# Plain fp32 products of the attentions held for a companion, and a charge for each change of product kind in the build's estimate

## The chip, the cores and the metric

The kernel runs on one core of one Trainium2 chip. The metric is device time in microseconds (us), and lower is better. In the text TensorE (PE) makes the matrix products, with its weight loads listed apart (PEld); VectorE is DVE, ScalarE is ACT, GpSimd is POOL, and SP is the engine whose queue starts most of the DMA transfers.

## The reference

One step of a one-layer decoder, on a prompt of 512 tokens and on 8 samples of 4 new tokens each, with the same weights. All data are fp32. Cut to what matters here:

```
z = rmsnorm(x) @ w_in                       # 2048 -> 7712 columns: q, k, v, gates
# group A, 8 heads, 2 shared k/v heads: native sparse attention
kc, vc = compress(rows of k, v)             # one row for each 32 tokens
o_A = g0*softmax(q kc) vc + g1*softmax(q k_selected) v_selected + g2*softmax(q k_window) v_window
# group B, 8 heads: forgetting attention
s[t, u] = q[t].k[u]/sqrt(128) + D[t] - D[u],  D = cumsum(log sigmoid(...))
o_B = softmax(s) v
y = rmsnorm(x + concat(o_A*silu(z_A), o_B*silu(z_B)) @ w_out)
```

The prompt attends to itself. A sample attends also to 1024 past tokens, which lie in pages of 128 rows in a shared cache and are found by a page table. The projected k and v, the logs of the forgetting gates and the new windows are outputs too.

## The kernel before

**The products.** The kernel has two kinds of matrix product. The projections, the compression and the prompt attentions split each operand into a high and a low part of type fp32r and make three products of them (`mm3`): high*high, high*low, low*high. In the profile they appear as `pz` (projections, output in PSUM), `s`, `psb` (compression), `s` and `tr` with inputs `nk`/`fk` (scores), `acc`, `accf` with `npt`/`fpt` (values). The sample attentions use plain fp32 products (`mm`), most with 32 columns of stationary data, and the profile lists two records for each of these: `accv<-ft,fqb` (forgetting scores against turned pages, 16 records for a half of a pair of pages), `accv<-fpg,fpt` (forgetting values, 8 records a page block), `s<-skt,qb` (selected and window scores of NSA, 32 records), `acc<-spg,PT` (their values, 8 records). Transposes are plain fp32 too and appear as `tr<-ident,...`, in blocks of one to five: `np` and `npc` for the NSA prompt's probabilities, `fp` for the forgetting prompt's, `fss` and `sp` for the samples', `zt` for the output.

**The order.** The order of all engines' instructions is found while the program is built, in Python. Each piece of work is a generator (a stream). `run_tiles` goes through the projections' 128-column tiles; a tile of the input projection has 32 `mm3` calls, 96 products, and after each `mm3` it calls `S.pump()`, which lets every stream go on that is ready. A stream says at each `yield` what it waits for: a list of tiles (ready when the estimate says so), names of flags (`"v7"` is set when the tile of that name was stored), or a test. `Clock` estimates when each instruction would run: it holds one time for each engine and adds a cost for each instruction and 0.25 us for a hop between engines. The projections thus fill TensorE between the steps of the attentions, and 61 tiles of the input projection come before those of the output.

**The streams.** `fox()` does, for each of two groups of four heads, `fox_sample` and then `fox_prompt`; it waits for the flags of the group's q, k and v tiles (`v0` to `v3`, `v4` to `v7`). `fox_prompt` is itself two streams: the scores, and `apply()`, which transposes the probabilities and multiplies them with the values. `nsa()` does `compress`, `nsa_prompt` (scores and `apply()` too) and `nsa_sample`. At the end it sets `mx`; `run_tiles` needs it before the output projection. There `mix` multiplies each head with its gate and `turn_in` writes it in two parts (`h_hi`, `h_lo`) over the first projection's input, once the input tiles are done.

Transposes, and some scores, go through two PSUM buffers called `tr`. A stream asks for one with `yield from S.take()`, whose test passes when a buffer is left and free, and gives it back with `S.put()`. The pages of `fox_sample` (`fpg`) have two buffers; `ahead()` starts the next load when one is released. The pages of `nsa_sample` (`spg`) have five.

Of the kernel before, what the change touches and what calls it, by code (L numbers as in the profile page):

```python
# [8 lines left out]
F32R = mybir.dt.float32r  # L9
# [30 lines left out]
class Clock:  # L40
# [2 lines left out]

    def __init__(self):
        self.t = dict(pe=0.0, dve=0.0, act=0.0, pool=0.0, sp=0.0)
        self.gate = {}
        self.bus = self.ring = 0.0
        self.slot, self.wr, self.rd, self.plane, self.parts = {}, {}, {}, {}, {}
        self.end = 0.0
        self.stall = {}  # L50
        self.who = ""
# [38 lines left out]
    def note(self, eng, op, a, k):  # L90
        aps = [x for x in a if isinstance(x, bass.AP)] + [k[n] for n in ("in_", "bias", "scale") if isinstance(k.get(n), bass.AP)]
        outs = []
        if "out" in k:
            outs.append(k["out"])
        else:
            outs.append(aps.pop(0))
        accum = k.get("accum_out")
        if accum is not None:
            outs.append(accum)
        start = self.t[eng]  # L100
        reads = [s for x in aps for s in self.keys(x)]
        writes = [s for x in outs for s in self.keys(x)]
        for s in reads:
            w = self.wr.get(s)
            if w:
                start = max(start, w[0] + (self.HOP if w[1] != eng else 0.0))
        for s in writes:
            for d in (self.wr, self.rd):
                w = d.get(s)
                if w and not ("dma" in op and w[1] == "dma"):  # L110
                    start = max(start, w[0] + (self.HOP if w[1] != eng else 0.0))
        dma = "dma" in op
        if eng == "pe" and start > self.t[eng] + 0.02:
            self.stall[self.who] = self.stall.get(self.who, 0.0) + start - self.t[eng]
        if dma:
            if eng == "pool":
                self.t[eng] = start = start + (1.25 if "indirect" in op else 0.75)
            else:
                self.ring = start = max(start, self.ring) + 0.47
                self.t[eng] += 0.06  # L120
            size = 4.0 * max(x.shape[0] * elems(x) for x in outs)
            self.bus = max(self.bus, start + 0.65) + size / 320e3
            end = self.bus + 2.2
            eng = "dma"
        else:
            end = start + self.cost(eng, op, outs[0], aps, accum is not None)
            self.t[eng] = end
            self.end = max(self.end, end + self.HOP)
        for s in reads:
            if s:  # L130
                self.rd[s] = max(self.rd.get(s, (0.0, 0)), (end, eng))
        for s in writes:
            if s:
                self.wr[s] = (end, eng)
# [45 lines left out]
        return max(self.clock.wr.get(k, (0.0, 0))[0], self.clock.rd.get(k, (0.0, 0))[0])  # L180


class Streams:

    AHEAD = 0.5

    def __init__(self, clock):
        self.clock = clock
# [2 lines left out]
        self.left = {"tr": 2, "nat": 2}  # L191

    def add(self, gen, front=False, filler=False):
        s = dict(gen=gen, flags=(), at=0.0, test=None, filler=filler)
        if front:
            self.items.insert(0, s)
        else:
            self.items.append(s)

    def pump(self):  # L200
        c = self.clock
        moved = again = False
        while True:
            again = False
            for s in list(self.items):
                now = c.t["pe"]
                if s["at"] > now or any(f not in self.flags for f in s["flags"]) or (s["test"] and not s["test"]()):
                    continue
                if s["filler"] and c.t["dve"] > now + self.AHEAD:
                    continue  # L210
                again = moved = True
                s["flags"], s["test"] = (), None
                c.end = now
                c.who = s["gen"].__name__
                try:
                    r = next(s["gen"])
                except StopIteration:
                    self.items.remove(s)
                    c.who = ""
                    continue  # L220
                c.who = ""
                s["at"] = now
                if isinstance(r, str):
                    s["flags"] = (r,)
                elif isinstance(r, tuple):
                    s["flags"] = r
                elif isinstance(r, list):
                    s["at"] = max(c.ready(x) for x in r)
                elif callable(r):
                    s["test"] = r  # L230
                elif not s["filler"]:
                    s["at"] = c.end
            if not again:
                return moved

    def take(self, n=1):
        yield lambda: self.left["tr"] >= n and all(self.psum.free_at("tr", 2, i) + 0.1 <= self.clock.t["pe"] for i in range(n))
        self.left["tr"] -= n

    def put(self, n=1):  # L240
# [33 lines left out]
def trunk_step(ctx, tc, x_prompt, x_sample, cache_nsa_kv, cache_fox_kv, cache_fox_logf, state_nsa_win,  # L274
# [27 lines left out]
    flags = S.flags  # L302
# [576 lines left out]
    def fox_sample(hh):  # L879
# [4 lines left out]
        pages, at = {}, [0, 0]  # L884
# [20 lines left out]
        s = fx.tile([P, 1056], F32, name="fss")  # L905
# [22 lines left out]
        for kq in range(2):  # L928
            acc = psum.tile([P, SEQ], F32, name="accv", tag="accv", bufs=1)
            for bq in range(2):  # L930
                for kp in range(2):
                    ts = [fx.tile([P, 2, 1024], F32, name="ft", bufs=2) for _ in range(2)]
                    for x in range(2):
                        pg = pages[at[1]]
                        for half in range(2):
                            yield [pg, ts[half]]
                            nc.vector.transpose(ts[half][:, x].rearrange("p (a d) -> p a d", d=64),
                                                pg.rearrange("p a (g d) -> p (a g) d", g=4)[:, :, half * 64:half * 64 + 64])
                        at[1] += 1
                        ahead()  # L940
                    for half in range(2):
                        yield [ts[half], acc]
                        scores(acc, half, bq, kp, ts[half])
            yield
            sl = s[:, kq * 512:(kq + 1) * 512]
            nc.vector.scalar_tensor_tensor(sl, acc, dcol, sl, op0=OP.add, op1=OP.add)
# [25 lines left out]
        pt = fx.tile([P, 1040], F32, name="fpt", tag="ft", bufs=2)  # L972
# [24 lines left out]
        for bq in range(2):  # L997
            vo = fx.tile([P, 1056], F32, name="fss")
            vsn, ob = vo[:32, :512], vo[:, 512:1024]
            load(vsn, dram(s_scr, hh * 4 * 4096, [[P, 32], [4096, 4], [1, P]]))  # L1000
            acc = psum.tile([P, SEQ], F32, name="accv", tag="accv", bufs=1)
            for kb in range(8):
                pg = pages.pop(at[1])
                yield [pg, pt, acc]
                for b in range(4):
                    o = kb * P + (bq * 4 + b) * 16
                    mm(acc[b * 32:b * 32 + 32], pt[:, o:o + 32], pg[:, b], kb == 0, False)
                at[1] += 1
                yield
                ahead()  # L1010
            yield [vsn, pn]
            for b in range(4):
                o = (bq * 4 + b) * 16
                mm(acc[b * 32:b * 32 + 32], pn[:, o:o + 32], vsn, False, True)
            yield
            cp(ob, acc)
            yield
            yield from S.take()
            tp = tr_tile([P, 4, P])
            for g in range(4):  # L1020
                nc.tensor.transpose(tp[:, g, :], ob[:, g * P:(g + 1) * P], ident)
            yield
            for g in range(4):
                nc.vector.tensor_copy(o_s[:, 8 + hh * 4 + g, bq * 16:bq * 16 + 16].rearrange("p (b t) -> p b t", t=4),
                                      tp[:, g, :].rearrange("p (b r) -> p b r", r=32)[:, :, g * 4:g * 4 + 4])
            S.put()
# [297 lines left out]
    def nsa_sample(pl):  # L1324
# [10 lines left out]
        sets, got = [], []  # L1335
# [29 lines left out]
        r = r.rearrange("p (a b) -> p a b", b=P)  # L1365
# [40 lines left out]
        for grp in range(2):  # L1406
# [78 lines left out]
            for br in range(2):  # L1485
                nk = 1024 if br == 0 else 512
                ps = [s_tile([P, SEQ]) for _ in range(nk // SEQ)]
                prev = None
# [13 lines left out]
                for half in range(nk // 256):  # L1502
# [3 lines left out]
                        nc.vector.transpose(kt[:, x], got.pop(0).rearrange("p a d -> p (a d)"))  # L1506
                        set_in()
                    if prev:
                        yield [prev[1]]
                        scores_of(*prev)  # L1510
                    prev = (half, kt)
                yield from S.take()
# [63 lines left out]
                values(k, [t[:, bb] for bb in range(4)], **kw)  # L1576
                set_in()
            for k in range(8):
                yield [got[0]]
                set_values(k, first=k == 0)  # L1580
            yield [vc]
            values(12, [vs] * 4, 64)
            values(13, [vc[:, grp, :]] * 4)
            for k in range(8, 12):
                yield [got[0]]
                set_values(k, last=k == 11)
            yield
            orw = T("sp", [P, 1024 + 64])[:, :256]
# [390 lines left out]
```

## Time and profile before

| | |
|---|---|
| median of 3 runs | 1355.34 us (1353.34 to 1359.38) |
| profiled execution | 1355.63 us, of which the span of the instructions is 1354.0 us |
| granted TensorE clock, mean | 0.983 of full speed |
| TensorE products | 1291.8 us busy (95%), 10597 records |
| TensorE weight loads | 1181.3 us (87%) |
| VectorE, ScalarE, GpSimd | 799.4 us (59%), 578.9 us (43%), 281.0 us (21%) |
| DMA | 276.02 MB, mean 204 GB/s |

The profile lists each instruction with its start and duration. Products overlap in the pipeline, so the distance from one start to the next is what a product costs in a stream of them, and its duration is longer. An idle time stands in square brackets with the instruction or transfer that ended it. Helpers make all instructions, so all have one line number (L146); they are told apart by the names of their tiles. Stretches are named by us from the span's start.

### The profile page before, as it was taken

How to read it: one execution, taken by the hardware profiler on the slowest of the kernel's cores; microseconds unless marked ns; L12 is line 12 of the kernel's file. 1: busy time of each engine (PE TensorE's matmuls, PEld its weight loads, DVE VectorE, ACT ScalarE, POOL GpSimd, SP SyncE). 2: the span in 40 equal slices, each digit the busy share in tenths (PEclk: the TensorE clock that was granted, in tenths of full speed). 3: DMA queues.
4: the chain of work that ended last, by engine and by line, in shares of the span. 5: the costliest groups of instructions: out<-in, count | busy, mean ns of one | idle time of the engine just before them, and what ended most of it. 6: DMA issues, size and time to landing. Idle time of an engine off the chain costs nothing.

```text
span 1354.0 us, 28683 instructions
## 1 busy us (share of the span) xinstructions
PE 1291.8 (95%) x10597; PEld 1181.3 (87%) x10597; DVE 799.4 (59%) x1988; ACT 578.9 (43%) x1319; POOL 281.0 (21%) x357
## 2 busy tenths in 40 slices
PE   6989999999998999999999998989999999999995
PEld 4889988889998879999988896756887998999995
DVE  5735778876644446666877854442675646343564
ACT  4313333244432345766543441322466634332563
POOL 3311367733200110000455301212112000000000
PEclk8999999999998999999999998989999999999998
DMA  7576699987646988457688748999897943333565
GB/s 194 148 193 175 187 265 297 270 242 214 172 105 157 307 276 249 139 153 229 202 239 252 217 105 197 285 275 322 224 228 231 298 147 110 109 99 109 148 197 189
DMA packets 383930, 276.02 MB, mean 204 GB/s; under 512 B 119667, under 2 KB 338659, under 8 KB 383117
## 3 DMA queue, kind: packets, MB, share of 16 engines
q1 hardware_dynamic: 359772, 198.09, 53.6%
q0 software_dynamic: 24016, 76.10, 18.1%
q8 instruction: 83, 1.36, 0.4%
q14 instruction: 59, 0.48, 0.1%
HBM read 241.82 MB, written 40.61 MB: 209 GB/s over the span
## 4 chain that ended last, share of the span: by engine, by line
PE 78%; DMA 10%; DVE 4%; SPq 3%; issue 2%; POOL 1%; ACT 1%; ACTq 0%; DVEq 0%; POOLq 0%
PE pz L146 57%; PE tr L146 5%; PE s L146 5%; PE accv L146 5%; PE acc L146 3%; DMA fpg<-in_cache_fox_kv,fi 3%; SPq L146 3%; DMA fpg<-in_cache_fox_kv 2%; PE psb L146 1%; PE accf L146 1%; DMA raw<-in_w_in 1%; DMA xt<-in_x_prompt 1%; POOL fpg L146 1%; DMA spg<-in_cache_nsa_kv 1%; PE pre L146 1%
## 5 line engine op out<-in xcount | busy, mean ns | idle before, releaser
L146 PE MATMUL pz<-h_hi,whi 128*128 128x272 f32 (+2 forms) x2432 | 720.3, 296 | 3.2 <-ACT whi L146 2.3
L146 PE MATMUL pz<-h_hi,wlo 128*128 128x272 f32 (+2 forms) x2432 | 704.8, 290 | 9.5 <-DVE wlo L146 9.5
L146 PE MATMUL pz<-h_lo,whi 128*128 128x272 f32 (+2 forms) x2432 | 702.4, 289 | 1.4 <-DVE h_lo L146 1.4
L146 PEld LDWEIGHTS pz<-h_hi,whi 128*128 128x128 f32 x2432 | 460.5, 189 | 38.5 <-issue 31.8
L146 PEld LDWEIGHTS pz<-h_hi,wlo 128*128 128x128 f32 x2432 | 459.2, 189 | 11.3 <-DVE wlo L146 11.2
L146 PEld LDWEIGHTS pz<-h_lo,whi 128*128 128x128 f32 x2432 | 461.1, 190 | 3.1 <-DVE h_lo L146 2.5
L146 ACT ACTIVATE whi<-raw 128x512 fp32r<-128x512 f32 x328 | 204.4, 625 | 264.5 <-PE pz L146 203.8
L146 DVE TENSOR_TENSOR wlo<-raw,whi 128x512 fp32r<-128x512 f32 x328 | 222.4, 679 | 137.4 <-ACT whi L146 127.9
L146 POOL DMA_INDIRECT fpg<-in_cache_fox_kv,fi x128 | 130.1, 1016 | 222.7 <-ACT nptch L146 144.8
L146 POOL DMA_INDIRECT crow<-in_cache_nsa_kv,ci x64 | 66.5, 1040 | 154.3 <-DVE ct L146 123.5
L146 DVE TENSOR_TENSOR zt<-pz,rsb 128x272 f32<-128x272 f32 x67 | 29.6, 441 | 107.1 <-PE pz L146 107.0
L146 DVE STREAM_TRANSPOSE ft<-fpg 128x1024 f32<-128x1024 f32 x64 | 78.5, 1231 | 22.5 <-DMA fpg<-in_cache_fox_kv,fi 22.4
L146 ACT ACTIVATE cxh<-ct 128x580 fp32r<-128x580 f32 (+1 forms) x64 | 42.3, 660 | 100.3 <-DVE ct L146 96.0
L146 POOL DMA_DIRECT2D fpg<-in_cache_fox_kv x64 | 35.3, 553 | 227.2 <-PE accv L146 166.0
L146 ACT ACTIVATE zt<-pz 128x272 f32<-128x272 f32 (+2 forms) x65 | 25.9, 398 | 113.3 <-PE pz L146 113.1
L146 POOL DMA_DIRECT2D spg<-in_cache_nsa_kv x64 | 35.0, 547 | 132.0 <-DVE skt L146 51.3
L146 DVE TENSOR_TENSOR cxl<-ct,cxh 128x580 fp32r<-128x580 f32 (+1 forms) x64 | 45.9, 717 | 10.1 <-ACT cxh L146 9.6
L146 PE MATMUL accv<-fpg,fpt 128*32 128x512 f32 x256 | 38.8, 631 | 10.5 <-DMA fpg<-in_cache_fox_kv 10.4
L146 ACT ACTIVATE npth<-tr 128x512 fp32r<-128x512 f32 x40 | 23.9, 596 | 49.6 <-PE tr L146 48.1
L146 DVE STREAM_TRANSPOSE ct<-crow 128x512 f32<-128x512 f32 x64 | 44.8, 700 | 0.0
L146 PE MATMUL accv<-ft,fqb 128*32 128x256 f32 x512 | 34.3, 385 | 4.6 <-DVE ft L146 4.6
L146 DVE CUSTOM_DVE_ANT_0 np<-s,nbias 128x128 f32<-128x128 f32 (+1 forms) x64 | 20.2, 352 | 30.7 <-PE s L146 30.7
(384 smaller groups left out, 1622.7 us busy)
## 6 DMA issues: line engine op xcount, KB each, us to landing
raw<-in_w_in SPq DMA_DIRECT2D x240, 256.0 KB
raw<-in_w_out SPq DMA_DIRECT2D x88, 256.0 KB
fpg<-in_cache_fox_kv SPq DMA_DIRECT2D x64, 256.0 KB
fpg<-in_cache_fox_kv POOLq DMA_DIRECT2D x64, 256.0 KB, 6.7
spg<-in_cache_nsa_kv POOLq DMA_DIRECT2D x64, 128.0 KB, 6.8
spg<-in_cache_nsa_kv SPq DMA_DIRECT2D x64, 128.0 KB
spg<-in_state_nsa_win SPq DMA_DIRECT2D x64, 128.0 KB
out<-in_state_nsa_win SPq DMA_DIRECT2D x32, 254.0 KB
```

Source lines behind the costliest of these rows:

```text
L146: return fn(*a, **k)
```

## The change

`Clock` keeps the kind of the last TensorE product in `mode` (true for fp32r) and adds 0.15 us to its estimate at each change of kind. Transposes count as plain.

A stream can now yield a `Soft` list, and the test of `take` is marked soft. A soft step that is ready while the last product was fp32r is held back: it goes on when a second stream's soft step is ready too, or when `PATIENCE`, 3 us of the estimate's TensorE time, has passed since it was first ready. While the last product was plain, soft steps go on at once. Soft are the two halves of the forgetting scores, the values of each page block, the NSA scores except the last of a branch, the NSA values, and every `take`: those ahead of transposes, those ahead of the fp32r scores of `fox_prompt` and of one part of `nsa_prompt`, and those of the output projection.

No product, transfer or buffer is added or removed.

```diff
 class Clock:
...
-        self.gate = {}
+        self.gate, self.mode = {}, False
...
+            if eng == "pe" and self.mode != (aps[0].dtype == F32R):
+                self.mode = not self.mode
+                start += 0.15; self.stall["sw"] = self.stall.get("sw", 0) + 1
             end = start + self.cost(eng, op, outs[0], aps, accum is not None)
...
+class Soft(list):
+    pass
...
     AHEAD = 0.5
+    PATIENCE = 3.0
...
+                if s["soft"] and c.mode:
+                    if s["soft"] is True:
+                        s["soft"] = now
+                    if now < s["soft"] + self.PATIENCE and sum(
+                            bool(x["soft"]) and x["at"] <= now and (not x["test"] or x["test"]()) for x in self.items) < 2:
+                        continue
...
                 elif isinstance(r, list):
-                    s["at"] = max(c.ready(x) for x in r)
+                    s["at"] = max((c.ready(x) for x in r), default=now)
+                    s["soft"] = isinstance(r, Soft) or None
                 elif callable(r):
                     s["test"] = r
+                    s["soft"] = getattr(r, "soft", None)
...
     def take(self, n=1):
-        yield lambda: self.left["tr"] >= n and all(self.psum.free_at("tr", 2, i) + 0.1 <= self.clock.t["pe"] for i in range(n))
+        free = lambda: self.left["tr"] >= n and all(self.psum.free_at("tr", 2, i) + 0.1 <= self.clock.t["pe"] for i in range(n))
+        free.soft = True
+        yield free
         self.left["tr"] -= n
...
# fox_sample
-                        yield [ts[half], acc]
+                        yield Soft([ts[half], acc])
                         scores(acc, half, bq, kp, ts[half])
...
-                yield [pg, pt, acc]
+                yield Soft([pg, pt, acc])
...
# nsa_sample
-                        yield [prev[1]]
+                        yield Soft([prev[1]])
                         scores_of(*prev)
...
-                yield [got[0]]
+                yield Soft([got[0]])
                 set_values(k, first=k == 0)
...
-                yield [got[0]]
+                yield Soft([got[0]])
                 set_values(k, last=k == 11)
```

More of the change, by code (lines that the diff above doesn't have):

```diff
@@ L193, in add @@
     def add(self, gen, front=False, filler=False):
-        s = dict(gen=gen, flags=(), at=0.0, test=None, filler=filler)
+        s = dict(gen=gen, flags=(), at=0.0, test=None, filler=filler, soft=None)
         if front:
@@ L211, in pump @@
                 again = moved = True
-                s["flags"], s["test"] = (), None
+                s["flags"], s["test"], s["soft"] = (), None, None
                 c.end = now
```

## The prediction

> **What bounds the kernel now.** I read the page first (span, busy shares), then busy time by stretch, then TensorE's instructions in order of time around single blocks, then the table of waits. All rows in these fences are: start us, duration us, engine, instruction, out<-operands, partitions*columns of the stationary side, shape of the moving side, count, and an idle time if there was one.
>
> ```profile
> span 1354.0 us, 28683 instructions
> ...
> PE 1291.8 (95%) x10597; PEld 1181.3 (87%) x10597; DVE 799.4 (59%) x1988; ACT 578.9 (43%) x1319; POOL 281.0 (21%) x357
> ```
> ```profile
> core 0: us, PE busy (x) PEld busy (x) DVE busy (x) ACT busy (x) POOL busy (x), PEclk, DMA share, GB/s
> ...
> 800.00:960.00 160.00, 146.81 (x1233) 111.83 (x1231) 62.68 (x184) 42.88 (x74) 38.34 (x70) 0.96 0.95 257
> 960.00:1082.00 122.00, 119.95 (x1068) 104.51 (x1067) 82.54 (x228) 78.01 (x158) 11.93 (x22) 1.00 0.88 243
> 1082.00:1137.00 55.00, 53.95 (x424) 53.11 (x423) 25.19 (x51) 21.03 (x36) 0.00 (x0) 1.00 0.48 141
> ```
>
> TensorE is the bound: it is busy 95% of the span and its granted clock is at or near 1. The projection's split products (`pz`) fill every moment in which no attention step is ready. So work on another engine matters only where TensorE waits for it, and an attention that gets later costs nothing until the projection runs out of tiles to fill with. In 1082:1137 the attentions are over and the projection still has 55 us of tiles: that is the reserve. Only 800:960, with the DMA engines at 0.95, shows a real hole on TensorE.
>
> **What a change of kind costs.** The edit rests on this price, so I took it from single blocks. In the last stretch above, nearly all `pz`, 424 records share 53.95 us, 0.127 each; between close neighbours it is 0.12 to 0.13, and I use 0.125 us for a step. Whatever a block adds beyond two such steps, between the last `pz` before it and the second one after it, is its full price.
>
> ```profile
> 697.35 0.29 PE L146 MATMUL pz<-h_hi,wlo 128*128 128x272 f32 x1
> 697.57 1.07 PE L146 MATMUL accv<-ft,fqb 128*32 128x256 f32 x16
> ...
> 698.80 0.29 PE L146 MATMUL pz<-h_lo,whi 128*128 128x272 f32 x1
> ...
> 700.44 0.28 PE L146 MATMUL pz<-h_hi,wlo 128*128 128x272 f32 x1
> 700.65 1.07 PE L146 MATMUL accv<-ft,fqb 128*32 128x256 f32 x16
> 701.65 0.66 PE L146 MATMUL tr<-ident,np 128*128 128x128 f32 x4
> ...
> 702.27 0.29 PE L146 MATMUL pz<-h_lo,whi 128*128 128x272 f32 x1
> ...
> 703.17 0.29 PE L146 MATMUL pz<-h_hi,wlo 128*128 128x272 f32 x1
> 703.30 0.60 PE L146 MATMUL tr<-ident,np 128*128 128x128 f32 x4
> ...
> 703.86 0.29 PE L146 MATMUL pz<-h_lo,whi 128*128 128x272 f32 x1
> ```
> ```profile
> 504.65 0.28 PE L146 MATMUL acc<-npth,nv1l 128*128 128x256 f32 x1
> 504.77 0.38 PE L146 MATMUL tr<-ident,npc 128*16 128x128 f32 x2
> ...
> 505.12 0.29 PE L146 MATMUL pz<-h_lo,whi 128*128 128x272 f32 x1
> ```
> ```profile
> 986.09 0.29 PE L146 MATMUL pz<-h_hi,wlo 128*128 128x272 f32 x1
> 986.31 1.93 PE L146 MATMUL s<-skt,qb 128*32 128x256 f32 x32
> ...
> 988.40 0.29 PE L146 MATMUL pz<-h_lo,whi 128*128 128x272 f32 x1
> ```
> ```profile
> 936.41 0.29 PE L146 MATMUL pz<-h_hi,wlo 128*128 128x272 f32 x1
> 936.63 0.64 PE L146 MATMUL acc<-spg,PT 128*32 128x256 f32 x8
> ...
> 937.42 0.29 PE L146 MATMUL pz<-h_lo,whi 128*128 128x272 f32 x1
> ```
>
> Four transposes: 703.86-703.17-0.25 = 0.44 us. Two: 505.12-504.65-0.25 = 0.22. That is 0.11 each with nothing left over: going from a split product to a transpose and back costs nothing. The products on 32 columns differ. Sixteen records (`ft`) cost 698.80-697.35-0.25 = 1.20; thirty-two of the same moving shape (`skt`) cost 988.40-986.09-0.25 = 2.06; eight (`spg`) 0.76. Two sixteens apart are 2.40 against 2.06 together, so joining two such blocks saves **0.34 us**. A sixteen with four transposes behind it costs 702.27-700.44-0.25 = 1.58 against 1.20+0.44 apart: 0.06 saved.
>
> ```profile
> 697.23 0.19 PEld L146 LDWEIGHTS pz<-h_hi,wlo 128*128 128x128 f32 x1
> 697.57 0.59 PEld L146 LDWEIGHTS accv<-ft,fqb 128*32 128x32 f32 x16
> 698.57 0.19 PEld L146 LDWEIGHTS pz<-h_hi,whi 128*128 128x128 f32 x1 [0.41 <-issue]
> ```
>
> The weight loads say where it goes: the load for the `pz` at 697.35 ran ahead of it, at 697.23, while the one for `ft` starts at 697.57 with its own product, and so does the next `pz`'s. [...]
>
> **The change, part by part.** No instruction is added or removed; TensorE's order changes, and with it the order on DVE, ACT and the DMA queues behind it.
>
> *Joins.* The groups give the number of 32-column blocks:
>
> ```profile
> L146 PE MATMUL accv<-fpg,fpt 128*32 128x512 f32 x256 | 38.8, 631 | 10.5 <-DMA fpg<-in_cache_fox_kv 10.4
> L146 PE MATMUL accv<-ft,fqb 128*32 128x256 f32 x512 | 34.3, 385 | 4.6 <-DVE ft L146 4.6
> L146 PE MATMUL acc<-spg,PT 128*32 128x256 f32 x192 | 14.5, 388 | 0.0
> ```
>
> `ft`: 512/16 = 32 blocks in 16 pairs, the halves one after the other. The quoted pair starts 3.08 us apart. Held 3 us, the first half runs when the second is about ready; after it the build's state is "plain", so the second goes at once, in the same block. Where the NSA attention's transposes are about (half of the second head group), the hold ends early and the pair stays apart: I count 14 of 16 joined. `spg`: 192/8 = 24, of which some already run four in a row; 18 stand alone, and since their generator yields nothing between two, a hold of 3 us collects two or three: 9 joins. `fpg`: 32 blocks, and a plain yield after each lets a `pz` in between, so they join only with another stream's; 3 more. 26 joins at 0.34 are **-8.8 us**; the ends are 14 (the pairs alone, -4.8) and 40 (-13.6). Joins with transposes: some 30 at 0.06 at most, -1.8, which I leave in the range.
>
> *Waits that a later place shortens.*
>
> ```profile
> PE accv L146 <- DMA fpg<-in_cache_fox_kv: 10.4, 2, 6.7
> PE accv L146 <- DVE ft L146: 4.6, 4, 1.6
> PE s L146 <- DVE skt L146: 2.7, 1, 2.7
> ```
>
> These seven waits (17.7 us) stand in front of steps that are now held. Up to 3 us each could go: 3+3+4.6+2.7 = -13.3 at most. But the page buffers are then released later and the next load starts later, and the heavier charge below pulls other steps forward in real time, which can make new waits of the same kind; the other end is +5, about half of the longest two here. I take -3.
>
> *The heavier charge.* Every change adds 0.15 us to the build's clock, 0.30 a block. For a transpose block the row says 0.00. There are 96/4+160/4+32/2 = 80 of them in the two prompt attentions (counted from the loops), so the build believes up to 24 us more TensorE time than passes. It costs nothing by itself; it brings dependent steps closer together in real time. ACT and DVE then have less margin (a quarter us per hop in the estimate); some short waits appear: +1.
>
> *The holds.* Who waits behind a held step: its own stream only, because the projection's products fill the place. The forgetting-attention chain is the longest: for each head group 18 held steps with the pages' values and their transposes, 13 with the scores and softmax, then 16 `take`s in the prompt's scores. These last ones are split products; holding them gains nothing. A hold lasts 0 to 3.4 us (3 plus one pumping step); among two or three streams I take half, 1.7. Values and scores are paced by page loads, so half of that counts: 15+11 us a group; the prompt's scores count fully, 27. The first group's scores and softmax are done before the projection has made `v3`, for which its values wait, and are left out. Where does the rest of the chain have room?
>
> ```profile
> 788.83 0.28 PE L146 MATMUL tr<-ident,fss 128*32 128x128 f32 x1
> ```
> ```profile
> 822.46 1.07 PE L146 MATMUL accv<-fpg,fpt 128*32 128x512 f32 x8
> ```
> ```profile
> 1083.72 0.28 PE L146 MATMUL accf<-fpth,fvl 128*128 128x256 f32 x1
> ```
> ```profile
> 1130.03 8.31 ACT L146 ACTIVATE h_hi<-mx 128x544 fp32r<-128x544 f32 x15
> ```
>
> The second group's softmax ends at 789 and its values start at 822, when the projection has made `v7`: 30 us of room. Delays ahead of it are 15+27+11 = 53, so 23 pass through; behind it 15+27 = 42. Together 65, less the 24 us by which the charge shortens the chain: 41. The last product of the chain ends at 1084 and the projection of the mixed heads begins at 1130: 46 us of room. The lateness is thus hidden, narrowly: **0**. If the page loads hide none of it, it is 108-24 = 84, which is 38 too late; that end goes to the rivals. The NSA chain ends before the forgetting one; its 48 held sample steps at 1.7 us, half of them paced by page loads and so halved, are some 40 to 60 us, less its share of the same 24: it has a little more room than it needs.
>
> *The sum.* -8.8-3+1 = -10.8 us. The profiled execution took 1355.63 us (span 1354.0), the median of the runs is 1355.34: about **1344.5 us**.
>
> **The rivals.** About 0.5% (6.8 us) is what can be told from no change here.
> - *The forgetting chain ends after the projection.* The attention's last heads are missing when the last input tile is done, and TensorE idles. It decides from 46 us of lateness on. For it: 16 prompt `take`s a group that hold split products, and the 0.95 DMA share, which leaves page loads no room to start later. Against it: nearly all of 163 to 1130 us has filler. Half way to the far end, 20 us too late: 1355.6-8.8+20 = 1367; the far end is 1385.
> - *Little happens.* Most companions are transposes, only the 14 `ft` pairs join, and the waits merely move: -4.8+1 = 1352. For it: 80 transpose blocks among the held steps.
> - *Joins and waits both go.* -13.6 and -10: 1332. Against it: the DMA share in 800:960.
>
> **How the numbers follow.** My forecast 0.43, with 1336 to 1348 as its own range; the first rival 0.23 (slower); little happens 0.24 (same); both go 0.10. So faster 0.53, same 0.24, slower 0.23. The range reaches from 1329, past the third rival, to 1373, past the middle of the first, and leaves out about 2 in 10.
>
> **What would show it.** Right: `accv<-ft` in blocks of x32, far fewer than 32 blocks of x16; single transpose blocks still at 0.44; waits for `fpg` and `skt` shorter; the last `accf` 30 to 45 us later and still ahead of the first `h_hi<-mx`. Wrong: a stretch with TensorE well under 0.9 between the last `pz` of the input tiles and `h_hi<-mx`; `ft` blocks still of x16; or new waits of several us for pages in 820 to 960.

## The result and the profile after

The changed kernel takes 1369.75 us (median of 5 runs, 1368.28 to 1374.6). The kernel before took 1359.38 us in the 5 runs beside it (1353.34 to 1360.88); the first three of these are the 1355.34 of the section above. The ratio is 1.0096, with a 95% interval of 1.0068 to 1.0125: slower, by about 13 us by the ratio (10 by the medians), where 10.8 us less were predicted. The profiled execution took 1369.46 us against 1355.63.

From the page of the changed kernel, span and busy shares:

```profile
span 1367.8 us, 28686 instructions
...
PE 1299.3 (95%) x10597; PEld 1186.4 (87%) x10597; DVE 802.0 (59%) x1995; ACT 578.9 (42%) x1319; POOL 277.3 (20%) x357
```

As many TensorE instructions as before, and the same share of a longer span. Its table of TensorE's waits, first the engine, the tile and line that waited, then what it waited for, us in total, times, longest:

```profile
PE accv L149 <- DMA fpg<-in_cache_fox_kv: 13.5, 6, 7.8
PE pz L149 <- DVE zt L149: 8.7, 1, 8.7
PE s L149 <- DMA kvc<-scr_kc: 4.4, 2, 2.7
...
PE pz L149 <- ACT zt L149: 2.8, 3, 2.1
```

And the `ft` group of the page, whose last number is its idle time:

```profile
L149 PE MATMUL accv<-ft,fqb 128*32 128x256 f32 x512 | 34.3, 385 | 0.4 <-DVE ft L149 0.4
```

The waits for `ft` went (4.6 to 0.4 us), those for pages grew (`fpg` 10.4 to 13.5), and one of 8.7 us is new, near the start.

To place the loss I took from each TensorE record the time to the next one's start and subtracted what it takes between close neighbours (0.124 us for a split product on 272 columns, 0.111 for a transpose, 0.054 or 0.107 for a record of a 32-column product on 256 or 512, and so on). What is left is called lost time; each column of the table counts from the mark of the column before. The 96 split products of each input tile of the projection serve as marks. Both kernels need 1213.5 us of such products. Chips B and C belong to the experiments below; no profile of the kernel before was taken on chip B, so its row from chip C stands for both.

| lost us up to input tile | 4 | 16 | 27 | 40 | 48 | 53 | end | sum |
|---|---|---|---|---|---|---|---|---|
| before, first chip | 27.2 | 13.4 | 15.1 | 12.2 | 30.9 | 10.5 | 14.5 | 124 |
| after, first chip | 36.1 | 9.1 | 10.6 | 13.0 | 38.1 | 14.9 | 15.4 | 137 |
| before, chip C | 25.5 | 64.4 | 15.7 | 29.7 | 33.4 | 11.6 | 14.1 | 194 |
| after, chip B | 36.4 | 60.7 | 12.9 | 37.6 | 46.9 | 14.5 | 15.3 | 224 |
| charge alone, chip B | 34.0 | 71.1 | 24.4 | 43.7 | 34.6 | 17.6 | 12.3 | 238 |
| holds alone, chip B | 28.1 | 58.4 | 16.7 | 18.8 | 32.9 | 21.8 | 23.9 | 201 |

The profiled execution of the charge alone was the longest of its six (1469.34 us, median 1459.38), so its sum is some 10 us high.

In the first pair the loss is 8.9 us in the first 106 us and 11.6 us between tiles 40 and 53 (about 746 to 1035 us); between tiles 4 and 27 the change gained 8.8. The early part can be read row by row. TensorE and DVE of the changed kernel:

```profile
84.33 0.29 PE L149 MATMUL pz<-h_hi,wlo 128*128 128x272 f32 x1
93.33 0.59 PE L149 MATMUL pz<-h_hi,whi 128*128 128x272 f32 x1 [8.71 <-DVE zt L149]
93.72 0.43 PE L149 MATMUL pz<-h_lo,whi 128*128 128x272 f32 x1
```
```profile
80.28 0.09 DVE L149 MEMSET more<- 128x32 f32 x1
91.10 1.25 DVE L149 STREAM_TRANSPOSE more<-cz 128x1024 f32<-128x1024 f32 x1 [10.67 <-DMA raw<-in_w_in]
92.27 0.65 DVE L149 TENSOR_TENSOR wlo<-raw,whi 128x512 fp32r<-128x512 f32 x1
92.84 0.43 DVE L149 TENSOR_TENSOR zt<-pz,rsb 128x272 f32<-128x272 f32 x1
```

And the same place before:

```profile
77.95 0.09 DVE L146 MEMSET more<- 128x32 f32 x1
85.15 1.25 DVE L146 STREAM_TRANSPOSE more<-cz 128x1024 f32<-128x1024 f32 x1 [7.06 <-DMA cz<-scr_n]
```
```profile
87.02 0.59 PE L146 MATMUL pz<-h_hi,wlo 128*128 128x272 f32 x1 [4.76 <-DVE wlo L146]
```

The evacuation `zt<-pz` at 92.84 could have run long before: no product ran between 84.62 and 93.33. It ran behind the transposes, in the order in which DVE's instructions were issued. (The transfer named behind the arrow is the one that landed last by the profile; the instruction reads `cz`.) So the transposes of the first sample cache wait for their load, and the weight split (`wlo`) and the evacuation (`zt`) that TensorE needs stand behind them. Before, DVE sat there 7.06 us; after, 10.67, and TensorE's wait went from 4.76 to 8.71 us. A smaller case of the same kind is on ACT, where a table load for the gates stands ahead of an evacuation:

```profile
54.40 1.28 ACT L149 ACT_TABLE_LOAD   x1 [2.33 <-issue]
55.70 0.24 ACT L149 ACTIVATE fpg<-fpg 128x40 f32<-128x40 f32 x1
55.84 0.38 ACT L149 ACTIVATE zt<-pz 128x272 f32<-128x272 f32 x1
```
```profile
56.27 0.39 PE L149 MATMUL pz<-h_hi,whi 128*128 128x272 f32 x1 [2.10 <-ACT zt L149]
```

The late part has page waits again, the longest where the second group's values are:

```profile
892.17 2.56 PE L149 MATMUL accv<-fpg,fpt 128*32 128x512 f32 x8 [7.81 <-DMA fpg<-in_cache_fox_kv]
```

### The profile page after: what moved, and what is told of

Its sections match the earlier page's. It is cut to its first block, busy times and chain, and to the rows that moved or that the text cites. A ratio compares the mean times of both kernels' runs of the same rounds, so it can differ in the third digit from the quotient of the medians.

```text
span 1367.8 us, 28686 instructions
## 1 busy us (share of the span) xinstructions
PE 1299.3 (95%) x10597; PEld 1186.4 (87%) x10597; DVE 802.0 (59%) x1995; ACT 578.9 (42%) x1319; POOL 277.3 (20%) x357
## 4 chain that ended last, share of the span: by engine, by line
PE 65%; DMA 15%; SPq 4%; DVE 4%; issue 3%; ACT 2%; POOL 1%; ACTq 0%; DVEq 0%; POOLq 0%
PE pz L149 48%; PE s L149 5%; SPq L149 4%; PE tr L149 4%; PE accv L149 3%; DMA fpg<-in_cache_fox_kv 3%; DMA fpg<-in_cache_fox_kv,fi 2%; PE acc L149 2%; PE psb L149 2%; DMA spg<-in_state_nsa_win 2%; DMA spg<-in_cache_nsa_kv 1%; DMA raw<-in_w_in 1%; POOL fpg L149 1%; PE accf L149 1%; DMA kvc<-scr_kc 1%
## 5 line engine op out<-in xcount | busy, mean ns | idle before, releaser
L149 DVE STREAM_TRANSPOSE ft<-fpg 128x1024 f32<-128x1024 f32 x64 | 78.4, 1231 | 24.2 <-DMA fpg<-in_cache_fox_kv,fi 24.0
L149 DVE TENSOR_TENSOR zt<-pz,rsb 128x272 f32<-128x272 f32 x60 | 26.4, 440 | 78.9 <-PE pz L149 78.5
L149 ACT ACTIVATE zt<-pz 128x272 f32<-128x272 f32 (+1 forms) x65 | 25.7, 395 | 93.7 <-PE pz L149 93.2
L149 PE MATMUL accv<-fpg,fpt 128*32 128x512 f32 x256 | 40.1, 619 | 13.5 <-DMA fpg<-in_cache_fox_kv 13.5
L149 ACT ACTIVATE np<-np,nst 128x128 f32<-128x128 f32 (+3 forms) x64 | 35.2, 552 | 10.1 <-DVE nst L149 10.1
L149 DVE STREAM_TRANSPOSE skt<-spg 128x1024 f32<-128x1024 f32 x24 | 29.0, 1231 | 16.8 <-DMA spg<-in_cache_nsa_kv 12.2
```

Of the source, the lines that this page charges most:

```text
L149: return fn(*a, **k)
```

## The experiments

They ran on five chips (named A, B, C, D, E here, one for each group of runs). On each of them the kernel before takes 1413 to 1428 us, where it took 1359 beside the first pair, whose chip is not on record and is called the first chip here. What differs in the traces is in the last section; why is not known. The times in the first expectations are meant for the first chip. Each ratio is to the kernel before on the same chip, so ratios can be compared, and times only within a chip. The theories: QUEUES (the holds move waiting instructions ahead of ready ones), CHARGE (the build believes TensorE later than it is), HOLDS (what is held feeds others late).

**The two parts, chip A.** The charge alone: the test for a hold becomes false.

```
-                if s["soft"] and c.mode:
+                if False and s["soft"] and c.mode:
```

> The changed kernel with the charge of 0.15 us for each change of kind and no holds. Three theories of the 12 us lost. QUEUES: the new order of issue puts instructions that wait ahead of ready ones on ACT, DVE and the load queue, in a few places (up to 106 us, and 820 to 1035 us); it is the holds that moved the gate stream there (its first transpose from 34.03 to 38.06 us). CHARGE: the build believes TensorE later than it is, so dependent steps come too close. HOLDS: steps that are held feed others late. CHARGE expects 1367 to 1371 us here, HOLDS and QUEUES (through the holds) 1354 to 1360, with the 2 us wait at 54 us for the evacuation on ACT gone.

Measured: 1455.42 us against 1418.3, ratio 1.0247 (1.021 to 1.0284). The charge alone is slow; the loss is about three times what CHARGE had expected (1367 to 1371 beside 1359 is 1.006 to 1.009).

The holds alone: the 0.15 is taken out of the clock, the change of kind is still followed.

```
-                start += 0.15; self.stall["sw"] = self.stall.get("sw", 0) + 1
+                self.stall["sw"] = self.stall.get("sw", 0) + 1
```

> The changed kernel with the holds and without the charge. HOLDS expects 1367 to 1371 us; CHARGE 1354 to 1358. QUEUES expects the wait behind the sample-cache transposes (8.7 us of TensorE at 84 us in the changed kernel) to stay only if the first sample loads are still issued at 80 us or later; then 1362 to 1370.

Measured: 1425.3, ratio 1.0037 (1.0011 to 1.0064). By the ratios the holds cost 5 us here and the charge 35 (by the medians 7 and 37). HOLDS falls as the main cause, though the 1.0037 lies between what it and CHARGE expected. QUEUES falls in the form I gave it: the early loss is there under the charge alone (34.0 us up to tile 4 in the table, against 25.5 before) and little of it under the holds (28.1), so it is the charge that moves the waiting instructions.

Both parts, but only from the setup of the forgetting attention's streams on (about 100 us), by a flag that the charge and the hold ask:

```
+        clock.on = True      # behind flags.add("fs_setup")
```

> The changed kernel with neither holds nor charge until the setup of the forgetting attention's streams is issued, so that the order of the first 100 us is the one of before. QUEUES expects the 8.9 us that the stretch up to the fifth input tile lost to come back and the rest to stay: 1359 to 1362 us. CHARGE and HOLDS, spread over all stages, expect 1366 to 1370.

Measured: 1443.53, ratio 1.0175 (1.0137 to 1.0213). Up to tile 4 the lost time is back at 25.3 us, as expected; the larger part of the loss comes later.

**The price of a join, chip A.** In the kernel before:

```
+                    yield [*ts, acc]
                     for half in range(2):
-                        yield [ts[half], acc]
                         scores(acc, half, bq, kp, ts[half])
```

> The kernel before, with one edit: the two halves of a block of the prompt's scores are both waited for ahead of the first, so that 16 pairs of x16 blocks on 32 columns become 16 blocks of x32. No hold, no charge. If the price of 0.34 us for a joined pair holds, 16 x 0.34 = 5.4 us less: about 1353 us beside 1359 for before. If the weight loads at the edges hide behind something else in the run, no change.

Measured: 1407.84, ratio 0.9916 (0.9885 to 0.9948), 12 us less. In a calm place of its trace a joined block stands so:

```profile
744.50 0.29 PE L146 MATMUL pz<-h_hi,wlo 128*128 128x272 f32 x1
744.72 1.93 PE L146 MATMUL accv<-ft,fqb 128*32 128x256 f32 x32
746.58 0.40 PE L146 MATMUL pz<-h_hi,whi 128*128 128x272 f32 x1
746.82 0.29 PE L146 MATMUL pz<-h_lo,whi 128*128 128x272 f32 x1
```

746.82-744.50-0.25 = 2.07 us, against 2 x 1.20 apart: 0.33 a pair, the price of the prediction. Sixteen pairs make 5.3 us. The interval is 7 to 16 us, so the joins save more than their edges; where the rest comes from was not traced to rows.

**The whole beside its parts, chip B.**

> The changed kernel itself, beside its two parts on one chip, since another chip gave 1418 us for the kernel before instead of 1359. All theories expect the ratio to before measured first, 1.007 to 1.013, if the loss is the kernel's; on a chip with slower transfers it may be more.

Measured: 1463.18 against 1427.82, ratio 1.0246 (1.0201 to 1.0292). The loss is larger than on the first chip, and outside the 1.007 to 1.013.

> The charge of 0.15 us for each change of kind alone, no holds, once more beside the whole change. CHARGE (the build believes TensorE later by 0.3 us at each of some 210 blocks, so dependent steps are issued too early): 1.010 to 1.025 of before, at least as slow as the whole change. HOLDS: 0.995 to 1.003.

Measured: 1459.38, ratio 1.0226 (1.0178 to 1.0274).

> The holds alone, no charge, once more beside the whole change. CHARGE: 0.997 to 1.004 of before. HOLDS: 1.007 or more.

Measured: 1433.96, ratio 1.003 (0.9996 to 1.0063). So on these chips the charge makes nearly all of the loss: with the holds in place, adding the charge costs 29 us (1463.18 against 1433.96).

The charge only at edges of 32-column products, no holds:

```
-            if eng == "pe" and self.mode != (aps[0].dtype == F32R):
+            if eng == "pe" and self.mode != (op != "transpose" and elems(aps[0]) == 32 and aps[0].dtype != F32R):
...
-                start += 0.15; ...
+                start += 0.07; ...
```

> No holds, and the charge only at the edges of products on 32 columns (0.07 us an edge, so that a block of 16 comes to the 1.20 us of the rows; transposes free). If it is the false charge on transposes that harms, 0.995 to 1.005 of before. If any change of the build's estimate scrambles the order as badly, 1.010 or more.

Measured: 1454.36, ratio 1.0171 (1.0119 to 1.0223), the second of the two. That the charge on transposes is false is not all that harms.

**A null run, the other sign and two repairs, chip C.**

> The kernel before, unchanged, for a profile beside the others on their chip and to see how far two builds of the same program differ. All theories: ratio 0.996 to 1.004.

Measured: 1426.72 against 1425.94, ratio 1.0004 (0.9983 to 1.0025). A quarter of one per cent can be told here.

The other sign: `start -= 0.07`, no holds.

> No holds, and the charge with the other sign: each change of kind takes 0.07 us off the build's clock for TensorE, some 420 changes, so 30 us of believed time less. If dependent steps come too early when TensorE is believed late (EARLY), this spreads them: 0.990 to 1.002 of before. If any change of the estimate spoils a good order (SCRAMBLE), 1.010 or more, as the small positive charge gave 1.017.

Measured: 1423.27, ratio 0.997 (0.9949 to 0.9991). Not every change of the estimate spoils the order; believing TensorE earlier at every change of kind does not harm.

The holds without the charge, and `yield Soft([*ts, acc])` ahead of both halves:

> The holds without the charge, and the two halves of a block of the prompt's scores waited for together, so that all 16 pairs join. Holds alone gave 1.003 and the pairs alone 0.992 of before: if the two add, 0.992 to 0.998; if holding a longer block makes the chain late, 1.003 or more.

Measured: 1416.94, ratio 0.9936 (0.9907 to 0.9966), as if the two added.

The pairs in the kernel before, and ahead of the first `more<-cz` a wait of 10 us of the build's TensorE time:

```
             yield [cz]
+            if kv == 0:
+                yield lambda t=clock.t["pe"]: clock.t["pe"] >= t + 10.0
```

> The kernel before, with the 16 pairs joined and with DVE's transposes of the first sample cache (more<-cz) put 10 us of the build's TensorE time later, behind the weights' splits that TensorE waits for at 80 to 90 us. Pairs alone 0.992; the wait there is 4.9 us in before: 0.987 to 0.991 if it goes, 0.992 if another wait takes its place.

Measured: 1433.39, ratio 1.0041 (1.0021 to 1.006): a miss. The table of waits gives 2.3 us for `wlo` where the kernel before has 5.3 on this chip, but up to tile 4 nothing is gained (26.5 us lost against 25.5), and between tiles 48 and 53 it loses 20.0 us against 11.6. Putting the sample stream later costs more than the early wait was worth; by which waits was not traced.

**How the loss follows the charge, chip D.** A third of it:

```
+                start += 0.05; ...
```

> No holds, the charge a third as large: 0.05 us for each change of kind. EARLY with a loss in proportion to the believed time: 1.006 to 1.010 of before (the full charge gave 1.023). If the loss comes as soon as the order differs at all: 1.015 or more. If it needs a threshold: 1.000 to 1.003.

Measured: 1435.64 against 1425.61, ratio 1.0057 (1.0027 to 1.0087), a hair under what a loss in proportion gives; the interval leaves out the 1.015 of a loss as soon as the order differs, but not the upper end of a threshold (1.003).

The full charge, no holds, with `HOP = 0.40` in place of 0.25:

> No holds, the full charge of 0.15 us, and the build's delay between engines raised from 0.25 to 0.40 us, so that a step that goes from TensorE over ACT and DVE and back is believed 0.45 us longer, somewhat more than the 0.30 us charged for its block. EARLY: the waits for nptl and npth at 575 to 852 us go and most of the loss comes back, 0.997 to 1.010. If what harms is the order itself, not the distance of dependent steps: 1.018 or more.

Measured: 1436.93, ratio 1.0086 (1.0052 to 1.0121). Some 60% of the loss under the charge alone (1.0226 on chip B) comes back when dependent steps are set further apart again. The longer hop was not run without the charge, so part of this gain may be its own. The waits on DVE for `nptl` show it in part. Charge alone on chip B, 575 to 852 us (input tiles 27 to 40):

```profile
PE tr L149 <- DVE nptl L149: 4.7, 1, 4.7
...
PE acc L149 <- DVE nptl L149: 2.7, 3, 2.2
PE acc L149 <- ACT npth L149: 1.8, 1, 1.8
```

The kernel before, chip C, and the run with the longer hop, over the same tiles:

```profile
PE tr L146 <- DVE fptl L146: 0.8, 1, 0.8
```
```profile
PE tr L149 <- DVE nptl L149: 2.8, 3, 1.7
```

Some 9 us of waits for the attention's own softmax parts are 0.8 before, and 2.8 with the hop. The longest one, 4.7 us, is no clean case, since DVE and ACT themselves stood still there (last section).

The full tables of TensorE's waits show more. Those on DVE and ACT add up to 18.8 us in the kernel before (chip C), to 44.6 and 42.1 under the charge alone (chips A and B), and to 18.1 with the charge and the longer hop. So some 24 us of the 32 to 37 that the charge alone costs are waits for these two engines. The distance of dependent steps moved the same way: in the forgetting prompt, the median time from the transposes of a block of probabilities to the value product that needs it is 3.80 us before, 2.95 under the charge alone on both chips, 4.02 with the longer hop and 4.17 with the negative charge. It is not all that counts, since with the longer hop 0.9% of loss remains.

Holds and charge only in the first 100 us, the flag turned the other way:

> Holds and charge as in the changed kernel, but only until the setup of the forgetting attention's streams is issued (the first 100 us); after that neither. The other half of the run with both only later (1.0175): if the parts add, 1.006 to 1.009, with the stretch up to the fifth input tile at 104 to 106 us instead of 96; if what is lost early is given back later, 1.000 to 1.003.

Measured: 1429.19, ratio 1.0034 (1.0008 to 1.006), between the two expectations. Up to tile 4 the trace loses 35.6 us against 25.5 for before; the time gives half of these 10 back. With the 1.0175 of the other half of the run the parts come to 1.021, inside the interval of the whole (these two halves ran on different chips).

The pairs with the negative charge, no holds:

> The pairs joined and the charge with the other sign (0.07 us off for each change), no holds. Alone they gave 0.992 and 0.997: if they add, 0.986 to 0.992; if they meet the same waits, 0.992 to 0.997.

Measured: 1402.18, ratio 0.9852 (0.9807 to 0.9896), as if the two added, or a little more. This version beats both kernels, by 23 us on its chip against before.

**The place of the charge, chip E.** The full 0.15 us only to and from transposes: `self.mode != (op == "transpose")`.

> No holds, 0.15 us charged only where TensorE goes to or from transposes, for which the rows show no price. If the loss follows the believed time (0.05 us gave 1.006, 0.15 us at all changes 1.023): half to two thirds of the full charge's, 1.010 to 1.016 of before. If it is the charge at the 32-column products that harms (0.07 us there alone gave 1.017): 1.000 to 1.005.

Measured: 1435.59 against 1413.37, ratio 1.0154 (1.012 to 1.0188), as a loss by believed time gives.

> No holds, 0.07 us taken off the build's clock at each edge of products on 32 columns, the opposite of the run that gave 1.017. If the sign decides: 0.988 to 1.000 of before. If any change at these places spoils the order: 1.008 or more.

Measured: 1428.37, ratio 1.0106 (1.0077 to 1.0134). At the 32-column products both signs cost over 1%. There the sign does not decide, and why is open: a changed estimate of exactly these blocks gives another order, and both orders that I tried are worse. In both the forgetting prompt's steps stand closer than before (3.47 us with +0.07, 3.30 with -0.07, against 3.80), so the distance goes with the loss here too, but the sign of the charge does not set it.

## Why the prediction was wrong

**Joins: the count failed, the price held.** 26 joins were predicted; the 32-column stretches I count in the two traces went from 97 to 90. The first step that failed is the sentence that after the first half the state is plain, "so the second goes at once, in the same block". Not one pair became a block of 32; two have only transposes between their halves. The first pair in the changed kernel:

```profile
176.62 0.28 PE L149 MATMUL pz<-h_hi,wlo 128*128 128x272 f32 x1
176.83 1.07 PE L149 MATMUL accv<-ft,fqb 128*32 128x256 f32 x16
177.83 0.40 PE L149 MATMUL s<-cxh,cwxh 128*128 128x290 f32 x1
...
181.58 0.29 PE L149 MATMUL pz<-h_hi,wlo 128*128 128x272 f32 x1
181.80 1.07 PE L149 MATMUL accv<-ft,fqb 128*32 128x256 f32 x16
```

The second half's list holds `acc` too, which the first half has just written. Its ready time is the end of that half plus the build's hop of 0.25 us, so it isn't ready at once, a split product goes in between, the state is split again, and the second half is held anew: the halves of this pair are now 4.97 us apart where they were 3.84, and over the 16 pairs the mean went from 2.93 to 3.97. The edge price of 0.34 us held (0.33 in the run of the pairs). At that price seven joins would give 2.4 us instead of 8.8.

What makes the edge cost is not settled, though. In the prediction's rows the sample attentions' products, which have 32 columns, pay it and the transposes do not. But the two transposes at 504.77 there have 16 columns and pay nothing (0.22 us for both), and neither does one on 32:

```profile
788.70 0.29 PE L146 MATMUL pz<-h_hi,wlo 128*128 128x272 f32 x1
788.83 0.28 PE L146 MATMUL tr<-ident,fss 128*32 128x128 f32 x1
...
789.06 0.29 PE L146 MATMUL pz<-h_lo,whi 128*128 128x272 f32 x1
```

789.06-788.70-0.25 = 0.11 us, the price of a transpose with nothing left over. So the rows show an edge price at the sample attentions' products alone; a small column count by itself cost these transposes nothing.

**Waits that a later place shortens: right for DVE, wrong for pages.** `ft` 4.6 to 0.4, `skt` 2.7 to nothing in the table, together 6.9 us gone. But `fpg` rose by 3.1, and `kvc`, 0.7 before, stands at 4.4, so the term comes to about 0 instead of -3. The prediction named this as what would prove it wrong, "new waits of several us for pages in 820 to 960", and gave it 5 us at most.

**The heavier charge: the step that decided on chips A and B, sized at +1 us.** On chip B it costs 31.6 us alone (1459.38 against 1427.82) and 29 us on top of the holds, on chip A 37 (all by the medians). Two things went wrong. The believed time was counted from 80 transpose blocks as 24 us; but every plain stretch is charged 0.30, and the trace has 171 of them: 51 us (213 and 64 us under the charge alone). Not all of it is false: at a half of the forgetting scores the build's own cost for the eight products is 1.06 us and the row's 1.20, so 0.14 of the 0.30 does pass. And "It costs nothing by itself" left out that the build sets each dependent step by that clock. Under the charge alone such steps came closer in real time, and TensorE's waits for DVE and ACT rose from 18.8 to 42 to 45 us: the "short waits" that the prediction saw coming, at some 24 us instead of 1.

The runs bear the direction out where the charge lies on all changes (-0.07: 0.997; 0.05: 1.006; 0.15: 1.023 to 1.025; compensated by the hop: 1.009) or on the transposes (1.015). For the 32-column places they do not.

For the whole change the path from the charge to the loss stays open. With the holds beside it the waits for DVE and ACT are 24.5 us on chip B. On the first chip they did not rise at all (26.5 us before, 24.2 after); there TensorE's waits for DMA rose, from 21.8 to 29.1 us. The parts were not run on the first chip, so that the charge makes the loss there too is inferred from chips A and B.

**The holds: the cover was there, the lateness was not.** The last products of the forgetting chain and the first step of the output projection after the change:

```profile
1091.72 0.28 PE L149 MATMUL accf<-fpth,fvl 128*128 128x256 f32 x1
```
```profile
1142.83 7.76 ACT L149 ACTIVATE h_hi<-mx 128x544 fp32r<-128x544 f32 x14
```

51 us of room, 46 before: nothing late, where 41 us were predicted. The `accf` come 8 us later, not 30 to 45; the NSA chain, which the prediction has ending first, ends 3 us behind them, at 1094.88. With the holds alone on chip B the chain ends at 1180.96 and the output projection begins at 1202.27, 21 us of room, where the kernel before has 46 (1154.50 to 1200.82, chip C). The room is the same on two chips wherever a kernel was profiled on two (46 us before, 51 after), so it belongs to the order. So the holds cost the chain 25 us, not 65, and the charge gives them back by pulling the chain forward. The first rival, the forgetting chain that ends after the projection, named the right side and the wrong cause; that its 1367 us lies near the 1369.75 is luck. The other rivals fall with the result.

**What no term had:** the early queues of DVE and ACT, shown above. The prediction looked at what is held, and not at what stands behind a waiting instruction in the first 100 us, where the projection's own splits share DVE with the sample caches.

## What to carry to other kernels

When a build orders work by an estimate, a term added to the estimate is a change of the whole order: test it alone, without the feature that it came with, even where rows show a price: 0.07 us at the 32-column edges, which the rows bear out, still cost 1.7%. To bring two steps together, wait for both inputs once ahead of both; a hold on each that waits for its predecessor's result separates them. A step that waits can do harm by what stands behind it in its engine's queue (here 10.67 us of DVE, and with them 8.71 of TensorE): look there for the wait of a slow load.

## What the hardware showed beside this

On chips A to E TensorE loses 52 to 71 us between tiles 4 and 16, on the first chip 9 to 13, for all kernels. The stretch 155 to 345 us of the kernel before, by stretch (busy us and counts of PE, PEld, DVE, ACT, POOL, then granted clock, DMA share, GB/s), first chip and then chip C:

```profile
155.00:345.00 190.00, 186.41 (x1587) 173.72 (x1586) 145.14 (x240) 68.39 (x146) 102.61 (x100) 1.00 0.87 250
```
```profile
155.00:345.00 190.00, 163.78 (x1179) 135.34 (x1178) 109.74 (x167) 45.85 (x93) 85.94 (x88) 0.88 0.69 201
```

TensorE's waits in it on chip C:

```profile
PE accv L146 <- issue: 10.9, 15, 1.5
PE s L146 <- issue: 9.4, 10, 2.0
PE pz L146 <- issue: 4.2, 8, 1.1
```

"Issue" is time in which nothing that the profile shows was waited for; over the whole kernel it is 34.5 us on chip C, and the first chip has none. These holes lie mostly where GpSimd issues its gathers, one after the other (about 1 us each): some 18 of the 26 us here. Of the lost time behind tile 4 chip C has 57 us inside such stretches and 112 outside, the first chip 15 and 82. Other engines stop too, in the charge run of chip B both at once:

```profile
796.78 0.42 DVE L149 CUSTOM_DVE_ANT_0 np<-s,nbias 128x256 f32<-128x256 f32 x1 [7.38 <-remote]
```
```profile
796.86 0.60 ACT L149 ACTIVATE npth<-tr 128x512 fp32r<-128x512 f32 x1 [7.18 <-remote]
```

On chip A the same two instructions of the charge alone stand still 7.28 and 7.09 us (at 786.65 and 786.73), so this standstill comes back with that order. Why these chips have the holes and the first has not was not settled. It may make the charge dearer there than on the first chip, so how the 1.0096 splits on the first chip itself is inferred, not measured by parts.

After the wait of 8.7 us at 84 us the products followed each other at about 0.226 us (93.72 to 94.85 is five steps) instead of 0.125, until about 98.5: this wait cost more than its length. That stretch and the one behind it, the granted clock after the POOL numbers:

```profile
93.30:100.00 6.70, 6.67 (x33) 6.67 (x34) 2.01 (x3) 0.63 (x1) 0.00 (x0) 0.59 0.58 100
100.00:106.00 6.00, 6.00 (x50) 6.00 (x49) 1.56 (x3) 1.26 (x2) 0.00 (x0) 1.00 0.70 177
```

The trace has two rates: 0.226 us a product, where the granted clock was 0.50 (93.30 to 98.50 us), and 0.125 us at 1.00 (100 to 106). The return took some 5 us here, and in the kernel before, behind its wait of 4.76 us, some 3 us (87.02 to about 90.2, at a granted clock of 0.50).
